# The feed-forward of a hybrid decoder block by one level of a Strassen scheme, up and down as two stages

## The chip, the cores and the metric

The kernel runs on one core of one Trainium2 chip. The metric is the device time of one execution in microseconds (us); of several runs the median is given. The core's engines each have a queue of their own and meet by semaphores: TensorE (PE) multiplies matrices into PSUM banks, VectorE (DVE), ScalarE (ACT) and GpSimd (POOL) work on tiles, and SyncE (SP) issues most of the DMAs.

## The reference, cut to what matters

The block has a norm, a wide input projection, three branches (a gated delta rule, a state space scan, a windowed attention), a gated merge and an output projection. The change lies behind all of these, in the last lines:

```python
h = h + merged @ w_out[l]
hn = rmsnorm(h, norm2_w[l])
h = h + jnp.square(jax.nn.relu(hn @ w_up[l])) @ w_down[l]
...
return rmsnorm(h, final_norm_w)[:, N_META:]
```

There are 1024 tokens (the meta tokens are not computed here), the model is 1024 wide and the feed-forward 4096, all in float32.

## The kernel before, in words

Every matmul operand is split into a high part, ScalarE's copy of the value in TensorE's fp32r type (`hi`, names that end in h), and the rest (`lo`, names that end in l); a product of two operands is three matmuls, hi x hi, hi x lo and lo x hi, that add up in one PSUM bank. A matmul here takes 128 partitions of both operands: 128 columns of the one by 512 of the other, into a bank of 128x512. Tokens come in two halves of 512, or eight tiles of 128 (NB = 8); the 1024 model channels in eight tiles of 128 (KT = 8) or two halves of 512; the 4096 channels of the feed-forward in 32 blocks of 128 (NFF = 32).

`stage_out` (L1083 on) makes h2, the residual with the output projection, in four rounds (token half `th`, column half `q`), each into four banks `pso` by 8 x 4 x 3 matmuls (L1108); VectorE adds each bank to h2 (L1112). In the round `th = 1, q = 0`, `mlp_in` is put between: for a token tile, ScalarE sums the squares (`row_scale`, L1125), VectorE adds and scales the sums (L1127, L1128) and takes the inverse (L1135), TensorE transposes the rows (`ups`, L1140), and ScalarE and VectorE make the transposed operand's hi and lo (L1144, L1145). The rows are not normalised for this; their factor `rs` is applied at the end, since the square of the relu scales with its square.

`stage_mlp` (L1148 on) goes over the 32 blocks two at a time, 16 passes. Up, 96 matmuls by `gemm` (L144): 2 blocks x 2 token halves x 3 x 8. Each of the four banks gets a relu (ACT, L1160), a square (DVE, L1161) and a split (ACT L1163, DVE L1164). Down, 96 matmuls (L1177): for each of 8 token tiles and 2 column halves, 2 blocks x 3; after each 6, VectorE adds the bank to h2, scaled by `rs` (L1179). Weights are split by ScalarE (L118, L131) and GpSimd (L120, L132). At the end `final_stats` and `final_apply` (L1197, L1204) normalise token tile by token tile and store; GpSimd makes the factor `rsf` as a power.

The order of the instructions on each engine is made by a scheduler with priorities and a cost model of its own; so the order in the source is not that on an engine, and the order is shown below. Tiles come from pools: a tag with a number of buffers, where a new tile waits until the last reader of the one before has ended. The eight PSUM banks are three pools: `mm` with three, `pc` with three, `pd` with two. A tag "y" has 32 buffers of 128x512, "m" 17, "d" 16, "t" and "r" four each; the eight h2 tiles are 128x1024. GpSimd's part in the merge and in the output projection (`wol`) is of the same form, L132.

## Time and profile before

| | us |
|---|---|
| median of three runs | 2766.83 (2761.62 to 2774.05) |
| the profiled execution | 2763.22 |
| its span, first to last instruction | 2761.5 |
| mean granted TensorE clock | 0.982 |
| up to the last round but one of the output projection | 1967.84 |
| last two rounds of the output projection | 48.3 |
| from there to the second pass of the feed-forward | 55.9 |
| the other passes, the norm and the stores | 689.5 |

From the second row on the times are those of the profiled execution. In its views each row has a start or a group, an engine, the line of the kernel and the names of the tiles (out<-in); "idle" in square brackets or behind the second bar is the time for which the engine waited before it, with what released it. A line L144 is that of the helper `gemm`; its tile's name, `up`, tells whose it is.

### The profile page before, as it was taken

The numbers are of one execution on the slowest core, as the hardware profiler recorded it, in microseconds if no ns is written. First come the engines' busy times: TensorE is split into PE (matmuls) and PEld (weight loads), VectorE is DVE, ScalarE is ACT, GpSimd is POOL, SyncE is SP. The second block draws the span as 40 slices with busy tenths as digits, with TensorE's granted clock in tenths as the row PEclk, the third lists the DMA queues.
The fourth block names the chain that finished last, engine by engine and source line by source line (L and its number), as shares of the span: only waits on it lengthen the run. The fifth ranks groups of instructions, "written<-read, shape, count | busy, mean of one in ns | idle before, by whom it ended". The sixth has DMA issues, their size and how long they took to land.

```text
span 2761.5 us, 36981 instructions
## 1 busy us (share of the span) xinstructions
PE 2629.8 (95%) x14367; PEld 2234.7 (81%) x14367; DVE 1456.6 (53%) x2775; ACT 906.1 (33%) x2385; POOL 696.3 (25%) x519
## 2 busy tenths in 40 slices
PE   6998999999999999999999999999999999999998
PEld 5887888888898898788878888888778777777776
DVE  5777766775665765576750122424254544444445
ACT  4434444443332332465541121212442121212122
POOL 3222222221232332322112222222432222222220
PEclk9989999998999999999999999999999999999999
DMA  3211121111112111322131131313221111111101
GB/s 120 64 42 53 52 60 52 53 44 49 47 62 85 62 62 62 88 61 63 47 122 46 54 106 46 107 53 114 90 73 54 39 53 44 50 47 51 47 16 69
DMA packets 88366, 172.94 MB, mean 63 GB/s; under 512 B 35862, under 2 KB 36278, under 8 KB 88190
## 3 DMA queue, kind: packets, MB, share of 16 engines
q1 hardware_dynamic: 83982, 162.81, 18.3%
q0 software_dynamic: 3200, 6.43, 1.1%
q8 instruction: 113, 1.85, 0.3%
q10 hardware_dynamic: 1008, 1.34, 0.1%
q14 instruction: 63, 0.52, 0.1%
HBM read 144.96 MB, written 19.14 MB: 59 GB/s over the span
## 4 chain that ended last, share of the span: by engine, by line
PE 75%; DVE 17%; issue 3%; ACT 2%; DMA 2%; POOL 1%; DVEq 0%; SPq 0%; POOLq 0%; ACTq 0%
PE up L144 13%; PE dn L1177 11%; PE mgm L144 9%; PE pr L1059 9%; PE pso L1108 3%; PE x L144 3%; PE gg L144 2%; PE aq L144 2%; PE v L144 2%; DVE xt L508 2%; PE z L144 2%; PE b L144 2%; PE q L144 1%; PE c L144 1%; PE k L144 1%
## 5 line engine op out<-in xcount | busy, mean ns | idle before, releaser
L1179 DVE SCALAR_TENSOR_TENSOR h<-dn,rs,h 128x512 f32<-128x512 f32 x256 | 191.9, 750 | 132.7 <-PE dn L1177 132.7
L1177 PE MATMUL dn<-wdh,ah 128*128 128x512 f32 x512 | 203.9, 398 | 14.9 <-DVE h L1179 14.9
L1161 DVE TENSOR_TENSOR ra<-ra 128x512 f32<-128x512 f32 x64 | 94.4, 1475 | 214.2 <-ACT ra L1160 214.2
L1177 PE MATMUL dn<-wdh,al 128*128 128x512 f32 x512 | 202.3, 395 | 0.0
L1177 PE MATMUL dn<-wdl,ah 128*128 128x512 f32 x512 | 202.2, 395 | 0.0
L1059 PE MATMUL pr<-yl,wph 128*128 128x512 f32 x384 | 150.1, 391 | 1.9 <-DVE yl L132 1.9
L1059 PE MATMUL pr<-yh,wph 128*128 128x512 f32 x384 | 150.1, 391 | 1.8 <-ACT wph L118 1.0
L132 POOL TENSOR_TENSOR wdl<-wdr,wdh 128x512 fp32r<-128x512 f32 x64 | 81.9, 1308 | 274.9 <-PE dn L1177 273.5
L1059 PE MATMUL pr<-yh,wpl 128*128 128x512 f32 x384 | 149.5, 389 | 0.0
L120 POOL TENSOR_TENSOR wul<-wur,wuh 128x1024 fp32r<-128x1024 f32 x32 | 76.6, 2393 | 249.7 <-PE up L144 246.7
L1177 PEld LDWEIGHTS dn<-wdh,ah 128*128 128x128 f32 x512 | 96.1, 188 | 45.6 <-DVE h L1179 23.9
L144 PE MATMUL up<-ul,wuh 128*128 128x512 f32 x512 | 129.0, 394 | 0.0
L144 PE MATMUL up<-uh,wul 128*128 128x512 f32 x512 | 128.4, 391 | 0.0
L144 PE MATMUL up<-uh,wuh 128*128 128x512 f32 x512 | 128.2, 391 | 0.0
L1069 DVE SCALAR_TENSOR_TENSOR gt<-gt,pr 128x512 f32<-128x512 f32 x32 | 21.9, 687 | 198.9 <-PE pr L1059 198.9
L131 ACT ACTIVATE wdh<-wdr 128x512 fp32r<-128x512 f32 x64 | 40.5, 633 | 255.5 <-PE dn L1177 246.6
L120 POOL TENSOR_TENSOR wpl<-wpr,wph 128x1024 fp32r<-128x1024 f32 x24 | 61.2, 2549 | 228.2 <-ACT wph L118 205.3
L1177 PEld LDWEIGHTS dn<-wdh,al 128*128 128x128 f32 x512 | 96.2, 188 | 23.3
L1177 PEld LDWEIGHTS dn<-wdl,ah 128*128 128x128 f32 x512 | 96.2, 188 | 21.8
L144 PEld LDWEIGHTS up<-ul,wuh 128*128 128x128 f32 x512 | 96.9, 190 | 20.0
L144 PEld LDWEIGHTS up<-uh,wul 128*128 128x128 f32 x512 | 96.4, 188 | 19.7
L144 PEld LDWEIGHTS up<-uh,wuh 128*128 128x128 f32 x512 | 96.1, 188 | 20.1
(422 smaller groups left out, 6563.2 us busy)
## 6 DMA issues: line engine op xcount, KB each, us to landing
wur<-in_wup SPq DMA_DIRECT2D x32, 512.0 KB
wdr<-in_wdn SPq DMA_DIRECT2D x64, 256.0 KB
mgr<-in_win SPq DMA_DIRECT2D x24, 512.0 KB
wpr<-in_wpr SPq DMA_DIRECT2D x24, 512.0 KB
yr<-yd SPq DMA_DIRECT2D x48, 256.0 KB
dms<-rowd SPq DMA_DIRECT2D x16, 512.0 KB
wor<-in_wout SPq DMA_DIRECT2D x32, 256.0 KB
gm<-rowd SPq DMA_DIRECT2D x8, 576.0 KB
```

The source lines that it names most:

```text
L120: nc.gpsimd.tensor_tensor(wl, wr, wh.bitcast(F32), op=ALU.subtract)
L131: nc.scalar.activation(h, r, AF.Copy)
L132: eng.tensor_tensor(l, r, h.bitcast(F32), op=ALU.subtract)
L144: nc.tensor.matmul(ps[:, 0:n], a[:, k, :], b[k][:, c0:c0 + n], start=(i == 0 and k == 0), stop=(i == 2 and k == KT - 1))
L508: nc.vector.tensor_tensor(tv, lb[:, j:j + 1, j + 1:32].broadcast_to([3 * n_, n, m]), ub[:, 0:n, j:j + 1].broadcast_to([3 * n_, n, m]), op= ...
L1059: nc.tensor.matmul(ps, x[:, k, :], y, start=(k == 0 and j == 0), stop=(k == KT - 1 and j == 2))
L1069: nc.vector.scalar_tensor_tensor(t, t, 1.0, ps, op0=ALU.add, op1=ALU.mult)
L1108: nc.tensor.matmul(ps, x[k, th][:, ts], y, start=(k == 0 and j == 0), stop=(k == KT - 1 and j == 2))
L1161: nc.vector.tensor_tensor(r, r, r, op=ALU.mult)
L1177: nc.tensor.matmul(ps, a[:, ts], b, start=(j == 0 and i == 0), stop=(j == G - 1 and i == 2))
L1179: nc.vector.scalar_tensor_tensor(self.h2[t][:, qs], ps, self.rs[:, t:t + 1], self.h2[t][:, qs], op0=ALU.mult, op1=ALU.add)
```

## The change

The two matrix products of the feed-forward become block products of 2 x 2 blocks, done with seven products in place of eight (Winograd's form of Strassen's scheme).

Up: two blocks of the feed-forward (a pair; 16 of them), two halves of the 1024 input channels, two halves of the tokens. A product is 12 matmuls of four channel tiles (`up_mm`); seven of them, `up1` to `up7`, make the four blocks c11, c12, c21, c22 of the pair. Their operands are sums and differences: of the activations, made once (`u_mix`, operand sets 0 to 6), and of the pair's weights, made anew for each pair (`ss`, `st`), on VectorE; all low parts of the up stage are made on VectorE. Since sums come after the transposes, the rows are now multiplied by their norm's factor before (`u_prep`: the power on GpSimd, the product on VectorE, L1169). Relu and square are both ScalarE's. The c's and four sums and differences of them, s1 to s4, seven tiles of 256 KB per pair, go to DRAM (`acd`) on SyncE's queue (`keep`, L1227). h2 is stored to DRAM (`hd`) and read back for the down stage, which gives its tiles to the weights. The first two products of pairs 0 and 1 are written ahead of `u_mix` (HOIST).

Down: three groups of 6, 5 and 5 pairs; in a group seven products, each a sum over its pairs, with operands read back from `acd` (L1357) and weights or differences of weights (`mix`); three of the seven make their weights' low part on GpSimd, the others on VectorE. A product fills four banks (one for each token tile of a half), 12 matmuls for each pair, and is then added to V, E7 or the h tiles (L1382). In the last product of all, the token tiles are the outer loop (`tail`).

The diff, cut to what is added in the place of `mlp_in` and of the body of `stage_mlp`, which calls `stage_up` and `stage_down` now; `h2tile`, `y2`, `m2`, `d2`, `t2` and `r2` take tiles of the tags above, `up_w1` loads a block of weights, `up_first` splits it, `up_hoist` does products 1 and 2, `relu2` is relu and square on ScalarE, `keep` stores to `acd`, `accum` adds four banks to each of the tiles that it is given (or, if `fresh`, copies them on ScalarE), and `bank` gives the four banks:

```diff
+NPR = NFF // 2
+HOIST = 2
...
+        self.acd = self.dram.tile([NPR, 7, P, 512], F32, name="acd")
+        self.hd = self.dram.tile([NB, P, D], F32, name="hd")
...
-                    if th == 1 and q == 0 and k % 2:
-                        self.mlp_in((k // 2,))
+                    if th == 1 and q == 0:
+                        if k == 0:
+                            self.u_prep(0)
+                        self.u_tile(0, k)
...
+    def split(self, src, hi, lo, eng=None):
+        nc = self.nc
+        nc.scalar.activation(hi, src, AF.Copy)
+        (eng or nc.vector).tensor_tensor(lo, src, hi.bitcast(F32), op=ALU.subtract)
+        return hi, lo
+    def u_prep(self, c):
+        nc = self.nc
+        self.hs = {}
+        for t in range(4 * c, 4 * c + 4):
+            nc.sync.dma_start(self.hd[t], self.h2[t])
+            r = self.final_stats(t)
+            if c:
+                w = self.h2tile("hs")
+                hs = [w[:, 0:512], w[:, 512:D]]
+            else:
+                hs = [self.y2("hs") for _ in range(2)]
+            for i in range(2):
+                nc.vector.tensor_scalar(hs[i], self.h2[t][:, 512 * i:512 * i + 512], r[:, 0:1], None, op0=ALU.mult)
+            self.hs[t % 4] = hs
+    def u_tile(self, c, k):
+        nc = self.nc
+        ps = self.pc("ups")
+        for t in range(4):
+            nc.tensor.transpose(ps[:, t * P:(t + 1) * P],
+                                self.hs[t][k // 4][:, (k % 4) * P:(k % 4 + 1) * P], self.ident)
+        n2 = self.cols[:, C_N2 + k:C_N2 + k + 1]
+        u = self.ur[c, k] = self.y2("u") if c == 0 else (self.t2 if k < 4 else self.r2)("u")
+        nc.scalar.activation(u, ps, AF.Copy, scale=n2)
+        if c == 0:
+            self.uo[0 if k < 4 else 1, k % 4] = self.split(u, self.y2("uh", F32R), self.y2("ul", F32R))
+    def u_mix(self):
+        nc = self.nc
+        b11, b12, b21, b22 = ([self.ur[c, 4 * i + k] for k in range(4)] for i in range(2) for c in range(2))
+        t2 = []
+        for k in range(4):
+            nc.vector.tensor_tensor(b11[k], b12[k], b11[k], op=ALU.subtract)
+        for k in range(4):
+            nc.vector.tensor_tensor(b12[k], b22[k], b12[k], op=ALU.subtract)
+        for k in range(4):
+            self.uo[2, k] = self.split(b22[k], self.y2("uh", F32R), self.y2("ul", F32R))
+            nc.vector.tensor_tensor(b22[k], b22[k], b11[k], op=ALU.subtract)
+            self.uo[5, k] = self.split(b22[k], self.m2("uh", F32R), self.d2("ul", F32R))
+        for k in range(4):
+            self.uo[4, k] = self.split(b11[k], self.m2("uh", F32R), self.d2("ul", F32R))
+        for k in range(4):
+            self.uo[6, k] = self.split(b12[k], self.m2("uh", F32R), self.d2("ul", F32R))
+        for k in range(4):
+            nc.vector.tensor_tensor(b21[k], b21[k], b22[k], op=ALU.subtract)
+            self.uo[3, k] = self.split(b21[k], self.m2("uh", F32R), self.d2("ul", F32R))
+    def up_mm(self, ps, w, p):
+        wh, wl = w
+        ops = [self.uo[p, k] for k in range(4)]
+        for j, (x, y) in enumerate(((wh, 0), (wh, 1), (wl, 0))):
+            for k in range(4):
+                self.nc.tensor.matmul(ps, x[:, k * P:(k + 1) * P], ops[k][y], start=(j == 0 and k == 0),
+                                      stop=(j == 2 and k == 3))
...
+    def up_pair(self, j, pre):
+        nc = self.nc
+        tt = nc.vector.tensor_tensor
+        w1 = self.up_w1(j)
...
+        if pre is None:
+            a11, a12 = self.up_first(w1)
+            pa = self.pd("up1")
+            self.up_mm(pa, a11, 0)
+        else:
+            pa, pb = pre
+        x1 = self.t2("x1")
+        nc.scalar.copy(x1, pa)
+        ss = self.h2tile("ss")
+        tt(ss[:, 0:512], a[2], a[3], op=ALU.add)
+        tt(ss[:, 512:D], ss[:, 0:512], a[0], op=ALU.subtract)
+        h, l = self.split(ss, self.h2tile("sh", dt=F32R), self.h2tile("sl", dt=F32R))
+        s1, s2 = (h[:, 0:512], l[:, 0:512]), (h[:, 512:D], l[:, 512:D])
+        if pre is None:
+            pb = bank("up2")
+            self.up_mm(pb, a12, 1)
+        c11 = self.y2("c11")
+        tt(c11, x1, pb, op=ALU.add)
+        self.relu2(c11, c11)
+        self.keep(j, 0, c11)
+        p6 = bank("up6")
+        self.up_mm(p6, s2, 5)
+        u2 = self.t2("u2")
+        tt(u2, x1, p6, op=ALU.add)
+        p5 = self.pc("up5")
+        self.up_mm(p5, s1, 4)
+        u4 = self.t2("u4")
+        tt(u4, u2, p5, op=ALU.add)
+        st = self.h2tile("st")
+        tt(st[:, 0:512], a[0], a[2], op=ALU.subtract)
+        tt(st[:, 512:D], a[1], ss[:, 512:D], op=ALU.subtract)
+        h, l = self.split(st, self.h2tile("sh", dt=F32R), self.h2tile("sl", dt=F32R))
+        s3, s4 = (h[:, 0:512], l[:, 0:512]), (h[:, 512:D], l[:, 512:D])
+        p7 = bank("up7")
+        self.up_mm(p7, s3, 6)
+        tt(u2, u2, p7, op=ALU.add)
+        c22 = self.y2("c22")
+        tt(c22, u2, p5, op=ALU.add)
+        self.relu2(c22, c22)
+        self.keep(j, 2, c22)
+        p3 = self.pc("up3")
+        self.up_mm(p3, s4, 2)
...
+        s = self.y2("s3")
+        tt(s, c11, c12, op=ALU.subtract)
+        self.keep(j, 5, s)
+        s = self.y2("s1")
+        tt(s, c12, c22, op=ALU.add)
+        self.keep(j, 3, s)
+        sq = self.y2("s2")
+        tt(sq, s, c11, op=ALU.subtract)
+        self.keep(j, 4, sq)
+        a22 = self.split(a[3], self.r2("wh", F32R), self.r2("wl", F32R))
+        p4 = self.pc("up4")
+        self.up_mm(p4, a22, 3)
+        c21 = self.y2("c21")
+        tt(c21, u2, p4, op=ALU.add)
+        self.relu2(c21, c21)
+        self.keep(j, 1, c21)
+        s = self.y2("s4")
+        tt(s, c21, sq, op=ALU.subtract)
+        self.keep(j, 6, s)
+    def stage_up(self):
+        self.u_prep(1)
+        pre = [self.up_hoist(0)]
+        for k in range(4):
+            self.u_tile(1, k)
+            self.u_tile(1, k + 4)
+        pre += [self.up_hoist(j) for j in range(1, HOIST)]
+        self.u_mix()
+        for j in range(NPR):
+            self.up_pair(j, pre[j] if j < HOIST else None)
+    def stage_down(self):
+        nc = self.nc
+        tt = nc.vector.tensor_tensor
+        V = [self.d2("V") for _ in range(4)]
+        E7 = [self.d2("E7") for _ in range(4)]
+        for t in range(NB):
+            self.h2[t] = self.h2tile(f"h3{t}")
+            nc.sync.dma_start(self.h2[t], self.hd[t])
...
+        for p0, n in ((0, 6), (6, 5), (11, 5)):
+            first, lastc = p0 == 0, p0 + n == NPR
...
+            for j in prs:
+                w = self.wst.tile([P, D], F32, name="wd1", tag=("wr", "wh", "wl")[nw % 3])
+                nw += 1
+                nc.sync.dma_start(w, self.I["wdn"][2 * j])
+                b1.append(w)
+            for j in prs:
+                for i, b in enumerate((b21, b22)):
+                    w = self.m2("wd2")
+                    nc.sync.dma_start(w, self.I["wdn"][2 * j + 1][:, 512 * i:512 * i + 512])
+                    b.append(w)
+            b11, b12 = [w[:, 0:512] for w in b1], [w[:, 512:D] for w in b1]
+            T1 = [self.y2("T1") for _ in prs]
+            def product(acc, ai, bs, mix=None, tail=False, eng=None):
+                ops = []
+                for i, j in enumerate(prs):
+                    if mix:
+                        mix(i)
+                    r = (self.t2 if i % 2 else self.r2)("ar")
+                    nc.sync.dma_start(r, self.acd[j, ai])
+                    ah, al = self.split(r, self.y2("ah", F32R), self.y2("al", F32R))
+                    wh, wl = self.split(bs[i], self.y2("wh", F32R), self.y2("wl", F32R), eng)
+                    ops.append((ah, al, wh, wl))
+                def mms(i, t):
+                    ah, al, wh, wl = ops[i]
+                    for m, (x, y) in enumerate(((ah, wh), (ah, wl), (al, wh))):
+                        nc.tensor.matmul(acc[t], x[:, t * P:(t + 1) * P], y,
+                                         start=(i == 0 and m == 0), stop=(i == n - 1 and m == 2))
...
+            ps = bank()
+            product(ps, 0, b11, eng=nc.gpsimd)
+            accum(ps, V, fresh=first)
+            accum(ps, C11)
+            ps = bank()
+            product(ps, 3, T1, mix=lambda i: tt(T1[i], b12[i], b11[i], op=ALU.subtract))
+            accum(ps, C12, C22)
+            ps = bank()
+            product(ps, 1, b21, eng=nc.gpsimd)
+            accum(ps, C11)
+            ps = bank()
+            product(ps, 6, b22, eng=nc.gpsimd)
+            accum(ps, C12)
+            ps = bank()
+            product(ps, 4, T1, mix=lambda i: tt(T1[i], b22[i], T1[i], op=ALU.subtract))
+            accum(ps, V)
+            if lastc:
+                for t in range(4):
+                    tt(C12[t], C12[t], V[t], op=ALU.add)
+            ps = bank()
+            product(ps, 5, b22, mix=lambda i: tt(b22[i], b22[i], b12[i], op=ALU.subtract))
+            accum(ps, E7, fresh=first)
+            if lastc:
+                fb = [self.d2("fnb") for _ in range(2)]
...
+                for t in range(4):
+                    tt(E7[t], E7[t], V[t], op=ALU.add)
+                    tt(C21[t], C21[t], E7[t], op=ALU.add)
+                    tt(C22[t], C22[t], E7[t], op=ALU.add)
+                for t in range(4):
+                    self.final_apply(t, self.final_stats(t), fb)
+            ps = bank()
+            product(ps, 2, b21, mix=lambda i: tt(b21[i], b21[i], T1[i], op=ALU.subtract), tail=lastc)
+            if not lastc:
+                accum(ps, C21)
+            else:
+                for t in range(4):
+                    tt(C21[t], C21[t], ps[t], op=ALU.add)
+                    self.final_apply(4 + t, self.final_stats(4 + t), fb)
```

How the order moves, at three places. First VectorE at the start of the up stage, where `ul` are low parts of the activations' sums, `st` a weight sum for product 7 of pair 0, `sl` its low part, and `wul`, `ss` belong to pairs 2 and 1:

```order
L1154 TENSOR_TENSOR ul_18785<-u_18294,uh_18784 128x512
L1154 TENSOR_TENSOR ul_18790<-u_18323,uh_18789 128x512
L1201 TENSOR_TENSOR u_18352<-u_18352,u_18668 128x512
L1262 TENSOR_TENSOR c11_18811<-x1_18802,up2_18601 128x512
L1268 TENSOR_TENSOR u2_18829<-x1_18802,up6_18816 128x512
L1154 TENSOR_TENSOR ul_18795<-u_18352,uh_18794 128x512
L1272 TENSOR_TENSOR u4_18844<-u2_18829,up5_18831 128x512
L1274 TENSOR_TENSOR st_18846<-wu1_18798,wu2_18800 128x512
L1275 TENSOR_TENSOR st_18846<-wu1_18798,ss_18804 128x512
L1154 TENSOR_TENSOR wl_18899<-wu2_18800,wh_18898 128x512
L1154 TENSOR_TENSOR sl_18850<-st_18846,sh_18849 128x1024
L1154 TENSOR_TENSOR wul_19053<-wu1_19048,wuh_19052 128x1024
```

Before, VectorE has only the second token half's low parts (`ul`, L1145) here; the sums and their low parts are new.

Second, SyncE between the last store of the up stage and the first operands of the down stage; before, SyncE here only has the weights of the passes, in turn:

```order
L116 DMA wur_21317<-in_wup 128x1024
L116 DMA wur_21323<-in_wup 128x1024
L129 DMA wdr_21749<-in_wdn 128x512
L129 DMA wdr_21755<-in_wdn 128x512
L129 DMA wdr_21761<-in_wdn 128x512
L129 DMA wdr_21767<-in_wdn 128x512
```

And now:

```order
L1227 DMA acd_98<-c21_21210 128x512
L1227 DMA acd_98<-s4_21215 128x512
L1346 DMA wd2_21266<-in_wdn 128x512
L1346 DMA wd2_21268<-in_wdn 128x512
L1346 DMA wd2_21270<-in_wdn 128x512
L1346 DMA wd2_21272<-in_wdn 128x512
L1346 DMA wd2_21274<-in_wdn 128x512
L1346 DMA wd2_21276<-in_wdn 128x512
L1357 DMA ar_21288<-acd_98 128x512
L1357 DMA ar_21298<-acd_98 128x512
```

The weight loads of the down stage stand ahead of the first operand `ar`, and that one reads from `acd`, which the rows above it write.

Third, VectorE at the end of the down stage. Before, the additions of the last pass alternate with the norm's work:

```order
L1179 SCALAR_TENSOR_TENSOR h_17702<-dn,rs_18104,h_17702 128x512
L1127 TENSOR_TENSOR ssm<-ss_23445 128x1
L1204 SCALAR_TENSOR_TENSOR h_17698<-h_17698,rsf,fnb 128x512
L1179 SCALAR_TENSOR_TENSOR h_17702<-dn,rs_18104,h_17702 128x512
L1128 TENSOR_SCALAR ssm<-ssm 128x1
L1204 SCALAR_TENSOR_TENSOR h_17698<-h_17698,rsf,fnb 128x512
```

Now the low parts of the last product's operands 1 to 4 (`al`, `wl`) stand behind the additions to E7 and to the h tiles, which wait for the product ahead of it:

```order
L1416 TENSOR_TENSOR E7_21223<-E7_21223,V_21219 128x512
L1416 TENSOR_TENSOR E7_21224<-E7_21224,V_21220 128x512
L1417 TENSOR_TENSOR h35_21236<-h35_21236,E7_21223 128x512
L1418 TENSOR_TENSOR h35_21236<-h35_21236,E7_21223 128x512
L1417 TENSOR_TENSOR h36_21238<-h36_21238,E7_21224 128x512
L1418 TENSOR_TENSOR h36_21238<-h36_21238,E7_21224 128x512
L1416 TENSOR_TENSOR E7_21225<-E7_21225,V_21221 128x512
L1154 TENSOR_TENSOR al_24046<-ar_24043,ah_24045 128x512
L1417 TENSOR_TENSOR h37_21240<-h37_21240,E7_21225 128x512
L1418 TENSOR_TENSOR h37_21240<-h37_21240,E7_21225 128x512
L1154 TENSOR_TENSOR wl_24050<-wd2_23199,wh_24049 128x512
L1154 TENSOR_TENSOR al_24057<-ar_24054,ah_24056 128x512
```

The E7 rows that begin this chain (L1382, four of them) stand a few rows higher, and five more low parts follow.

More of the change, by code (lines that the diff above doesn't have):

```diff
@@ L1112, in stage_out @@
                     nc.vector.scalar_tensor_tensor(sl, ps, 0.5, sl, op0=ALU.mult, op1=ALU.add)
-                if th == 0 and q == 1:
-                    self.u = [[[self.half("y", 4 * KT, n) for n in ("uh", "ul")] for k in range(KT)]
-                              for c in range(2)]
-                    self.rs = self.lp.tile([P, NB], F32, name="rs2")
-        self.mlp_in(range(4, 8))
     def row_scale(self, t):
@@ new lines, in h2tile, with y2, m2, d2 @@
+    def h2tile(self, name, shape=(P, D), dt=F32):
+        return self.rp.tile(list(shape), dt, name=name, tag="h2", bufs=NB)
+    def y2(self, name, dt=F32):
+        return self.half("y", 4 * KT, name, dt)
+    def m2(self, name, dt=F32):
+        return self.half("m", NM, name, dt)
+    def d2(self, name, dt=F32):
+        return self.half("d", 2 * KT, name, dt, self.rp)
+    def t2(self, name, dt=F32):
+        return self.half("t", 4, name, dt, self.tp)
+    def r2(self, name, dt=F32):
+        return self.half("r", 4, name, dt)
@@ new lines, in up_mm, with up_w1 @@
+    def up_mm(self, ps, w, p):
[5 more added lines that the diff above has]
+                                      stop=(j == 2 and k == 3))
+    def up_w1(self, j):
+        w1 = self.wst.tile([P, D], F32, name="wu1", tag="wr")
+        self.nc.sync.dma_start(w1, self.I["wup"][2 * j])
+        return w1
@@ new lines, in up_first, with relu2, keep, up_hoist @@
+    def up_first(self, w1):
+        h, l = self.split(w1, self.wst.tile([P, D], F32R, name="wuh", tag="wh"),
+                          self.wst.tile([P, D], F32R, name="wul", tag="wl"))
+        return (h[:, 0:512], l[:, 0:512]), (h[:, 512:D], l[:, 512:D])
+    def relu2(self, dst, src):
+        self.nc.scalar.activation(dst, src, AF.Relu)
+        self.nc.scalar.activation(dst, dst, AF.Square)
+    def keep(self, j, i, src):
+        self.nc.sync.dma_start(self.acd[j, i], src)
+    def up_hoist(self, j):
+        pa = self.pd("up1")
+        a11, a12 = self.up_first(self.up_w1(j))
+        self.up_mm(pa, a11, 0)
+        pb = self.pmm.tile([P, 512], F32, name="up2", tag="mm", bufs=3)
+        self.up_mm(pb, a12, 1)
+        return pa, pb
@@ L1194, in final_stats @@
+    def stage_mlp(self):
+        self.stage_up()
+        self.stage_down()
     def final_stats(self, t):
```

100 lines of the change are left out of this document (40 added, 60 removed).

## Prediction

> **What bounds the kernel now.** I read the page's first and fourth part, then the chain of waits, then groups of instructions. The page gives busy time by engine and the chain's shares:
>
> ```profile
> PE 2629.8 (95%) x14367; PEld 2234.7 (81%) x14367; DVE 1456.6 (53%) x2775; ACT 906.1 (33%) x2385; POOL 696.3 (25%) x519
> PE 75%; DVE 17%; issue 3%; ACT 2%; DMA 2%; POOL 1%; DVEq 0%; SPq 0%; POOLq 0%; ACTq 0%
> ```
>
> TensorE is busy 95% of the span and holds 75% of the chain; VectorE is busy only 53%. The change touches the feed-forward, so its stretch matters. The chain there, in order of time (start, us, what):
>
> ```profile
> 1995.97 18.10 PE pso L1108 x79
> 2016.16 4.16 DVE ssm L1127
> ...
> 2072.02 21.80 PE up L144 x96
> ...
> 2253.76 21.80 PE up L144 x96
> 2276.26 2.35 DVE ra L1161
> 2279.33 19.86 PE dn L1177 x84
> 2299.19 21.80 PE up L144 x96
> ```
>
> One pass over two of the 32 blocks goes from 2253.76 to 2299.19, 45.43 us, for 192 matmuls. The windows view of the steady stretch (sum, then busy time of PE, PEld, DVE, ACT, POOL, then granted clock, DMA share, GB/s) says the same:
>
> ```profile
> 2072.02:2708.09 636.07, 622.17 (x2690) 502.82 (x2689) 290.09 (x336) 131.43 (x193) 137.04 (x83) 1.00 0.14 44
> ```
>
> TensorE is busy 622 of 636 us at full clock, the other engines less than half, the DMA 14%. Only fewer matmuls shorten this stretch, and the change takes away one in eight.
>
> **The gain.** Before, 16 passes have 192 matmuls each. After, each pair of blocks has 7 products of 12 matmuls in the up stage and 84 in the down stage: 168. In the chain an up matmul takes 21.80/96 = 0.2271 us, and one of the down projection 19.86/84 = 0.2364. The new up stage has the old one's form: 84 x 0.2271 = 19.1 us a pair. The new down stage sends three matmuls to a bank and then goes to the next of four, with no eviction between; nearest is the output projection, which does the same: 18.10/79 = 0.2291, so 84 x 0.2291 = 19.2 us. Per pair 38.3 instead of 45.43, 7.1 less; times 16, **-114 us** (-117 with the down stage at 0.2271, -104 at 0.2364).
>
> **Does TensorE stay the bound in the up stage?** The groups that price the new work:
>
> ```profile
> L1161 DVE TENSOR_TENSOR ra<-ra 128x512 f32<-128x512 f32 x64 | 94.4, 1475 | 214.2 <-ACT ra L1160 214.2
> L1164 DVE TENSOR_TENSOR al<-ra,ah 128x512 fp32r<-128x512 f32 x64 | 44.3, 693 | 33.0 <-ACT ah L1163 32.5
> L1069 DVE SCALAR_TENSOR_TENSOR gt<-gt,pr 128x512 f32<-128x512 f32 x32 | 21.9, 687 | 198.9 <-PE pr L1059 198.9
> L627 DVE TENSOR_TENSOR vt<-vt,f 128x1024 f32<-128x1024 f32 x8 | 9.8, 1226 | 13.9 <-POOL f L626 13.9
> L205 DVE TENSOR_SCALAR xn<-xt,xrs 128x1024 f32<-128x1024 f32 x4 | 3.0, 742 | 1.3 <-POOL xrs L201 1.3
> L131 ACT ACTIVATE wdh<-wdr 128x512 fp32r<-128x512 f32 x64 | 40.5, 633 | 255.5 <-PE dn L1177 246.6 <-DMA wdr<-in_wdn 6.1
> L1160 ACT ACTIVATE ra<-up 128x512 f32<-128x512 f32 x64 | 38.3, 598 | 178.5 <-PE up L144 178.5
> L118 ACT ACTIVATE wuh<-wur 128x1024 fp32r<-128x1024 f32 x32 | 33.9, 1060 | 24.7 <-PE up L144 24.7
> ```
>
> A pair gives VectorE 16 operations of 128x512 at 0.69 and three of 128x1024 at 1.23: 14.7 us. ScalarE has three hi parts at 1.06, one at 0.63 and nine copies, relus and squares at 0.60: 9.2 us. Both are under 19.1. In the order of the changed kernel, VectorE makes the weight sums of pair j+1 between the evictions of pair j, so TensorE never waits for a sum of its own pair. SyncE has seven stores and two loads a pair, 2.75 MB in 19.1 us or 144 GB/s, where a window of the clock's table below has 264. In the up stage GpSimd does almost nothing, which matters because of the first row's mean, 1475 against 693. The timeline shows both cases:
>
> ```profile
> 2265.39 0.69 DVE L1161 TENSOR_TENSOR ra<-ra 128x512 f32<-128x512 f32 x1 [3.35 <-ACT ra L1160]
> 2270.23 2.39 POOL L120 TENSOR_TENSOR wul<-wur,wuh 128x1024 fp32r<-128x1024 f32 x1 [12.95 <-PE up L144]
> 2270.83 2.35 DVE L1161 TENSOR_TENSOR ra<-ra 128x512 f32<-128x512 f32 x1 [3.36 <-ACT ra L1160]
> ```
>
> Alone it takes 0.69; beside a GpSimd operation it ends only after that one. An operation with a PSUM operand (L1069, 687 ns) isn't held up. I take 19.1 us for a pair.
>
> **The start of the up stage.** Before, from 2016.16 to 2072.02 are 55.9 us, of which 45.4 are a pass: 10.4 us over. After, two waits come. First, in the last output rounds TensorE transposes rows that are normalised already, so it waits for Squares, sums, a power and two multiplications:
>
> ```profile
> L1125 ACT ACTIVATE sqm<-h 128x512 f32<-128x512 f32 x32 | 20.0, 627 | 12.8 <-DVE ssm L1127 4.4 <-DVE ssm L1128 3.5 <-DVE h L1179 3.0
> L1125 ACT ACTIVATION_READ_ACCUMULATOR sqm<-h 128x1 f32 x32 | 6.0, 187 | 0.0
> L1127 DVE TENSOR_TENSOR ssm<-ss 128x1 f32<-128x1 f32 x16 | 6.6, 411 | 3.1 <-ACT sqm L1125 3.0
> L1128 DVE TENSOR_SCALAR ssm<-ssm 128x1 f32<-128x1 f32 x16 | 2.4, 150 | 0.3
> L1197 POOL TENSOR_TENSOR rsf<-ssm,pneg 128x1 f32<-128x1 f32 x8 | 5.5, 689 | 64.6 <-DVE ssm L1128 64.6
> L132 POOL TENSOR_TENSOR wol<-wor,woh 128x512 fp32r<-128x512 f32 x32 | 41.8, 1310 | 57.1 <-ACT woh L131 57.1
> ```
>
> For the last token tile: 2 x (0.63 + 0.19) + 0.41 + 0.15 + 0.69 + 2 x 0.37 = 3.6 us, and a wol of 1.31 may stand ahead on GpSimd. I take **+3.5** (0 if queued matmuls cover it, 6 with two wols). Second, the activations' combinations. The four last token tiles need 4 x 1.63 us of Squares on ScalarE, then 0.56 + 0.69 + 0.74, with 0.7 for the eviction ahead (it reads PSUM, like L1069): 9.2; a transposed round and its copy 1.2 more. Then 46 operations stand on VectorE in order until the low part for product 7 of pair 0: 44 x 0.69 + 2 x 1.23 = 32.8. So product 7 starts 43 us after the output projection, and eight products of the two first pairs follow, 96 matmuls or 21.8 us: 65 us, of which two pairs are 38.1. 27 us over against 10.4 before: **+16.6** (+8 if half of VectorE's row is done earlier than I think, +26 if the second pair's loads, which stand in SyncE's row behind pair 0's first store, come late). The hoisted products of pairs 0 and 1 are in the 43.
>
> **From up to down.** SyncE issues the last store, six weight loads, and only then the first read of what was stored. The merge stage's loads of the same 256 KB from DRAM price it; the issue rate is that of the loads of x:
>
> ```profile
> 1890.75 3.83 SPq L1088 DMA_DIRECT2D h<-in_x  x8
> ```
> ```profile
> 1425.89 4.51 DMA yr<-yd
> 1431.81 3.78 DMA yr<-yd
> 1437.68 3.46 DMA yr<-yd
> ```
>
> After the last product: sum 0.69, relu and square 1.2, s4 0.69, together 2.6; seven issues of 3.83/8 = 0.48, 3.4; the landing 4.5; the hi part 0.63: **+11.1** (8 if the landing takes 3.5 and issues go ahead, 16 if the 1.8 MB ahead drain first). The later operands follow at 0.48 us and are used at 2.7 us each, so they don't wait.
>
> **The down stage.** A group of six pairs has 118 operations of 0.69 on VectorE, 81 us, and 504 matmuls, 115 us; of five, 77 and 96. GpSimd makes 48 low parts of 1.31 in all. Added whole to VectorE (24 and 20 us a group) they come to 105 and 97: level with TensorE in the groups of five. **+3** (0 if the look-ahead of five to six items hides it, 25 if two fifths of the 63 us of holds land on the path). The Trainium skill, "SBUF — State Buffer", says of the port pair that the two engines share that it is an exclusive lock, that only VectorE operations with two SBUF inputs meet it here, and that whoever starts second waits in full. The three timeline rows and L1069 agree; by that rule alone the accumulations, which read PSUM, are never held, and this term would be 0 as long as the look-ahead covers the low parts.
>
> **The end.** In VectorE's order the low parts of the last product's operands 1 to 4 stand behind the sums that wait for the product ahead of it. From that product's end the last low part is the 24th operation: 24 x 0.69 = 16.6 us; 31 matmuls are then left, 7.1. Undisturbed the product is 60 x 0.229 = 13.7. 16.6 + 7.1 - 13.7 = **+10** (4 if more is ready, 15 since two operand loads also stand behind eight output stores). The tail:
>
> ```profile
> 2751.87 0.40 PE L1177 MATMUL dn<-wdh,al 128*128 128x512 f32 x1
> 2757.08 1.41 DVE L1204 SCALAR_TENSOR_TENSOR h<-h,rsf,fnb 128x512 f32<-128x512 f32 x2 [0.72 <-POOL rsf L1197]
> ```
>
> Before, 9.2 us from the last matmul to 2761.5. After, for one token tile: 0.69 + 1.63 + 0.56 + 0.69 + 1.41 and the same 3.0 of storing: 8.0, **-1**.
>
> **The clock.** A wait of TensorE in the timeline, and windows of 2 us around its end, with the columns as above:
>
> ```profile
> 2021.49 0.33 PE L1140 MATMUL ups<-ident,h 128*128 128x128 f32 x1 [3.88 <-DVE ssm L1128]
> ```
> ```profile
> 2020.00:2022.00 2.00, 0.51 (x3) 0.47 (x4) 1.82 (x9) 0.15 (x1) 0.30 (x1) 1.00 0.72 264
> 2022.00:2024.00 2.00, 2.00 (x9) 1.48 (x8) 1.31 (x6) 1.88 (x7) 0.00 (x0) 0.65 0.40 137
> 2024.00:2026.00 2.00, 2.00 (x8) 1.51 (x7) 0.60 (x4) 1.46 (x7) 0.00 (x0) 0.50 0.00 0
> 2026.00:2028.00 2.00, 2.00 (x11) 1.44 (x9) 1.07 (x6) 1.02 (x4) 0.00 (x0) 1.00 0.00 0
> ```
>
> After 3.88 us idle the granted clock is 0.65 and 0.50 for two windows: 0.7 + 1.0 = 1.7 us lost, about 2. The change has three more such waits: **+6** (2 to 8).
>
> **The sum.** -114 + 3.5 + 16.6 + 11.1 + 3 + 10 - 1 + 6 = -65. The profiled execution took 2763.2 us (span 2761.5); 2763.2 - 65 = 2698. The median of the runs lies 3.6 above that execution: **2702 us**. The terms' bounds, which seldom fall all to one side, make 2684 to 2728 of it.
>
> **The rivals.** *Almost the whole gain.* The lower bounds hold at the seams and TensorE fills them: -117 + 8 + 8 + 4 + 2 - 1 = -96, **2671**. For it: seven eighths of the matmuls are all the chain needs. Against: the orders show VectorE's and SyncE's rows as they are.
>
> *No change.* All 48 low parts of GpSimd in the down stage come onto the path, 48 x 1.31 = 63 us, and use up the 65: **2765**. For it: L1161 at 1475 instead of 693, and the sums of five pairs being level. Against: only three of seven products use GpSimd, and accumulations read PSUM, like L1069.
>
> *Slower: the up stage at VectorE's pace.* If its 22 units of a pair cost what L1161 does on average, 22 x 1.475 = 32.5 us, a pair takes 13.4 more than TensorE's 19.1; 14 pairs, +188: **2890**. It decides from 19.1 + 65/14 = 23.7 us a pair. Against: that mean comes from GpSimd, which is idle there.
>
> *Slower: the clock falls at every product of the down stage.* If each of the 21 products begins with a wait like the one of 3.88 us, it costs that and some 2 us of half clock: 21 x 5.9 = 124, **2826**; it decides from 11 of them. Against: operands are made five to six items ahead. The Trainium skill, "TensorE: Matmul & The Clock Gate", describes such an oscillation for matmul bursts that each wait for a load (the section on HAM oscillation); in this trace only single waits show it.
>
> That the matmuls aren't saved I rule out: the changed order has 84 a pair in each stage.
>
> **How the numbers follow.** Forecast 0.68, almost the whole gain 0.17, no change 0.07, slower by VectorE 0.04, slower by the clock 0.04. The first two and their bounds give the range 2664 to 2742, leaving out the rest and their fringes. About 0.5% (14 us) is what a measurement of this kernel can tell from no change: faster 0.85, same 0.07, slower 0.08.
>
> **What would show it.** Right: two products of pairs 2 to 15 in the chain 19.1 us apart from pair to pair; TensorE idle once some 11 us before the first down matmul, some 25 us in pieces before pair 2, some 10 us in the last product. Wrong: pairs over 20 us in the up stage; VectorE's two-input operations above 0.69 there; TensorE idle at most product changes of the down stage; down matmuls over 0.235.

## The result and the profile after

| | before | after | ratio, 95% interval |
|---|---|---|---|
| first measurement, median of four runs each (us) | 2765.05 | 2701.54 | 0.976 [0.973, 0.979] |
| the changed kernel again, median of eleven (before) and six runs | 2769.64 | 2697.73 | 0.973 [0.970, 0.976] |
| profiled execution of the first measurement, span | 2761.5 | 2698.7 | |
| from the output projection's first matmul to the end | 838.3 | 766.6 | |

The change is faster by 2.4 to 2.7%. The forecast was 2702, but the last row of the table says that this is a little too good to be true: the part of the program that the change touches became 72 us shorter, not 65, and the part ahead of it, whose code is the same, happened to take 9 us longer in the profiled execution of after. The first matmul of the output projection in the two timelines, before and after:

```profile
1923.21 0.39 PE L1108 MATMUL pso<-woh,mh 128*128 128x512 f32 x1
```
```profile
1932.12 0.39 PE L1115 MATMUL pso<-woh,mh 128*128 128x512 f32 x1
```

In the fourteen traces of this study that matmul begins between 1923 and 1944 us, whatever the kernel. So all that follows is measured from it; two traces of each kernel agree on that stretch within 1 us (838.3 and 839.2 before, 766.6 and 766.5 after).

The page of after, first and fourth part:

```profile
PE 2547.8 (94%) x13983; PEld 2178.5 (81%) x13983; DVE 1608.3 (60%) x3039; ACT 1034.7 (38%) x2581; POOL 614.7 (23%) x479
PE 75%; DVE 16%; issue 3%; DMA 2%; ACT 2%; POOL 1%; ACTq 0%; SPq 0%; DVEq 0%; POOLq 0%
```

TensorE has 384 matmuls less and is still the engine that is always busy; VectorE went up by 152 us and isn't the bound. The chain of waits through the feed-forward (start, us, what) shows its new form, two long runs of TensorE with a few waits at the seams, the places where one stage hands over to the next:

```profile
2027.84 1.80 DVE h L1119 x3
2051.90 5.32 DVE ul L1154 x9
2064.47 291.96 PE up L1209 x1260
2364.08 4.60 DMA wd<-in_wdn
2368.74 5.01 DMA ar<-acd
2375.10 291.63 PE dn L1365 x1274
2677.80 6.76 PE dn L1365 x22
```

TensorE's timeline at the beginnings of two pairs of the up stage, and then at its end and the seams that follow:

```profile
2204.86 1.07 PE L1209 MATMUL up<-uh,wuh 128*128 128x512 f32 x4
2224.13 1.07 PE L1209 MATMUL up<-uh,wuh 128*128 128x512 f32 x4
```
```profile
2064.47 2.07 PE L1209 MATMUL up<-uh,sh 128*128 128x512 f32 x4 [5.65 <-ACT sh L1153]
...
2358.12 1.09 PE L1209 MATMUL up<-uh,wl 128*128 128x512 f32 x4
2373.74 0.80 PE L1365 MATMUL dn<-wh,ah 128*128 128x512 f32 x1 [14.53 <-ACT wh L1153]
2375.10 0.80 PE L1365 MATMUL dn<-wl,ah 128*128 128x512 f32 x1 [0.56 <-POOL wl L1154]
...
2677.80 0.79 PE L1365 MATMUL dn<-wl,ah 128*128 128x512 f32 x1 [5.42 <-DVE wl L1154]
...
2689.15 0.39 PE L1365 MATMUL dn<-wh,al 128*128 128x512 f32 x1
```

A pair takes 2224.13 - 2204.86 = 19.27 us, and so do the pairs around it. The up stage ends at 2359.04 (the last four matmuls begin at 2358.12, 0.23 apart). The numbers in brackets are TensorE's waits: 5.65 for the first pair's weight sums (four of 0.75 to 2.01 stand ahead of it), 14.53 before the down stage, 5.42 in its last product; the down stage has no other above 0.6. Two windows, one pair of the up stage and the steady part of the down stage (sum, then PE, PEld, DVE, ACT, POOL, granted clock, DMA share, GB/s):

```profile
2166.31:2185.59 19.28, 19.28 (x86) 15.77 (x85) 13.64 (x19) 9.02 (x14) 0.00 (x0) 1.00 0.38 150
```
```profile
2380.00:2640.00 260.00, 260.00 (x1147) 215.36 (x1146) 212.27 (x304) 117.01 (x205) 65.37 (x45) 1.00 0.44 142
```

TensorE fills both; a matmul takes 260/1147 = 0.2267 us in the second. VectorE has 5.6 us of a pair to spare in the up stage, and 48 of 260 us in the down stage.

### The profile page after: what moved, and what is told of

The parts are those of the page before. It is cut to its first block, busy times and chain, and to the rows that moved or that the text cites. A ratio compares the mean times of both kernels' runs of the same rounds, so it can differ in the third digit from the quotient of the medians.

```text
span 2698.7 us, 37432 instructions
## 1 busy us (share of the span) xinstructions
PE 2547.8 (94%) x13983; PEld 2178.5 (81%) x13983; DVE 1608.3 (60%) x3039; ACT 1034.7 (38%) x2581; POOL 614.7 (23%) x479
## 4 chain that ended last, share of the span: by engine, by line
PE 75%; DVE 16%; issue 3%; DMA 2%; ACT 2%; POOL 1%; ACTq 0%; SPq 0%; DVEq 0%; POOLq 0%
PE dn L1365 11%; PE up L1209 11%; PE mgm L148 9%; PE pr L1063 9%; PE pso L1115 3%; PE aq L148 3%; PE x L148 3%; PE gg L148 2%; PE v L148 2%; PE q L148 2%; DVE xt L512 2%; PE z L148 2%; PE b L148 2%; PE c L148 2%; PE k L148 1%
## 5 line engine op out<-in xcount | busy, mean ns | idle before, releaser
L1365 PE MATMUL dn<-wh,ah 128*128 128x512 f32 x448 | 175.5, 393 | 14.5 <-ACT wh L1153 14.5
L1365 PE MATMUL dn<-wl,ah 128*128 128x512 f32 x448 | 176.2, 394 | 6.0 <-DVE wl L1154 5.4
L1365 PE MATMUL dn<-wh,al 128*128 128x512 f32 x448 | 175.6, 392 | 0.0
L1154 DVE TENSOR_TENSOR al<-ar,ah 128x512 fp32r<-128x512 f32 x112 | 98.7, 884 | 51.3 <-ACT ah L1153 51.1
L1365 PEld LDWEIGHTS dn<-wh,ah 128*128 128x128 f32 x448 | 85.1, 190 | 32.9 <-ACT wh L1153 15.0
L1365 PEld LDWEIGHTS dn<-wl,ah 128*128 128x128 f32 x448 | 85.1, 190 | 24.7 <-DVE wl L1154 6.1
L148 PE MATMUL mgm<-hnh,mgh 128*128 128x512 f32 x384 | 100.1, 398 | 2.1 <-ACT gt L1047 2.1
L148 PE MATMUL mgm<-hnl,mgh 128*128 128x512 f32 x384 | 99.9, 399 | 0.0
L148 PE MATMUL mgm<-hnh,mgl 128*128 128x512 f32 x384 | 99.5, 396 | 0.0
L1365 PEld LDWEIGHTS dn<-wh,al 128*128 128x128 f32 x448 | 85.2, 190 | 17.7
```

Source lines behind the costliest of these rows:

```text
L148: nc.tensor.matmul(ps[:, 0:n], a[:, k, :], b[k][:, c0:c0 + n], start=(i == 0 and k == 0), stop=(i == 2 and k == KT - 1))
L1154: (eng or nc.vector).tensor_tensor(lo, src, hi.bitcast(F32), op=ALU.subtract)
L1365: nc.tensor.matmul(acc[t], x[:, t * P:(t + 1) * P], y, start=(i == 0 and m == 0), stop=(i == n - 1 and m == 2))
```

## The experiments

The theory: TensorE is the bound in both stages, so each loses what its matmuls lose; what is given back stands at the seams, and each seam is the order of one engine's row. The rivals were VectorE as the bound of the up stage, GpSimd's holds on VectorE in the down stage, and transfers. All differences below are of the stretch from the output projection's first matmul to the end, against 766.6 us of the changed kernel, which takes the chance of the stages ahead out. Each comes from one trace of the edited kernel.

**Undo one half: the down stage with eight plain products.**

```diff
-            product(ps, 0, b11, eng=nc.gpsimd)
-            accum(ps, V, fresh=first)
...
+            for ai, bs, C, eng in ((0, b11, C11, nc.gpsimd), (0, b12, C12, None), (1, b21, C11, nc.gpsimd),
+                                   (1, b22, C12, None), (3, b11, C21, nc.gpsimd), (3, b12, C22, None),
+                                   (2, b21, C21, nc.gpsimd), (2, b22, C22, None)):
...
+                product(ps, ai, bs, eng=eng, tail=last)
...
-        tt(s, c11, c12, op=ALU.subtract)
-        self.keep(j, 5, s)
```

> The down stage with eight plain block products in place of seven, and without the sums s1 to s4; the up stage stays as changed. If the time of the down stage is that of its matmuls: 16 x 12 = 192 more at 0.227 us, +43.6 us, less up to 7 us because the sums at the end go, so about 37 to 44 us over the changed kernel (2738 to 2745). If the stage is paced by its loads or by VectorE and GpSimd, the seven products have not gained so much and it is under +20 us (below 2722).

Measured: 2739.87, the stretch 810.3, **+43.7**. The 192 matmuls more are 43.5 at 0.2266. Its waits sit elsewhere (7.0 us in the first product, and 10.0 in the fifth of the last group's eight, where this version puts the loads of the operands behind the stores of finished tokens) but sum to 18.9 us against 20.5. The down stage is paced by its matmuls, and its share of the gain is nearly whole.

**Undo the other half: the up stage with eight plain products.**

```diff
+                ps = self.pmm.tile([P, 512], F32, name="up", tag="mm", bufs=3)
+                for m, (x, y) in enumerate(((0, 0), (0, 1), (1, 0))):
+                    for k in range(KT):
+                        nc.tensor.matmul(ps, ws[k // 4][x][:, (k % 4) * P:(k % 4 + 1) * P],
+                                         self.uo[7 * c + k // 4, k % 4][y], start=(m == 0 and k == 0),
...
-        self.u_mix()
```

> The up stage with eight plain block products (96 matmuls a pair), without the sums of activations and weights; the stores and the down stage stay as changed. If the start of the up stage pays for the sums: 21.8 for 19.27 us a pair, +40, and the start goes from 22.8 us over two pairs back to about 10.6, -12, so about +28 us over the changed kernel (2730). If the start's waits come from something else (the norm, the transposes, the loads), +40 (2742).

Measured: 2716.82, the stretch 780.95, **+14.4**, less than either number. The up stage itself, from the end of the output projection, takes 355.7 us for 331.2: +24.5, near the +28, of which the pairs, 21.91 us each, are +42.2 and the start -17.7; its start has no wait over 0.4. The other 10 us come back at the seam to the down stage:

```profile
2385.20 2.00 PE L1213 MATMUL up<-uh,wul 128*128 128x512 f32 x8
2389.58 0.60 PE L1285 MATMUL dn<-wh,ah 128*128 128x512 f32 x1 [2.39 <-ACT wh L1153]
```

There TensorE waits 2.4 us where the changed kernel waits 14.5. So of the 42 us that fewer matmuls save in the up stage, two thirds go for the start and the seam; the sums cost more than I had put down for the start alone, and of the 58 us that the two halves bring one by one, three quarters are the down stage's. The other 14 of the 72 belong to neither alone. Two plain stages together weren't run, but the traces say where such a remainder comes from. Before, the 96 down matmuls of a pass took 45.43 - 21.80 = 23.63 us with their waits; in the new form 96 of them take 96 x 0.2266 = 21.75, which is 30 us less over 16 passes (a plain up pair takes 2 us more in all than before, 21.91 for 21.80). So of the 114 us that the pairs gain, some 86 (42.2 + 43.5) come from seven products in place of eight, and the other 28 from giving the down projection a stage of its own; by this estimate eight products would have had those 28 too, and paid the seams for them.

**Double the suspect: more sums on VectorE.** The four weight sums are repeated, 18 and then 6 operations more a pair:

```diff
         tt(ss[:, 0:512], a[2], a[3], op=ALU.add)
+        tt(ss[:, 0:512], a[2], a[3], op=ALU.add)
...
         tt(st[:, 0:512], a[0], a[2], op=ALU.subtract)
+        tt(st[:, 0:512], a[0], a[2], op=ALU.subtract)
...
```

> Each pair of the up stage repeats its four weight sums, 18 more operations of 128x512 on VectorE; the results are the same. If TensorE is the bound at 19.27 us and VectorE has room: its row a pair is 13.2 us at the spacing of 0.61 (14.7 at 0.69), so with 18 more 24.2 to 27, and the pairs take that: +4.9 to +8 us a pair, +70 to +110 us. If VectorE's row already sets the pace, all 18 count: 18 x 0.61 x 16 = +176 us. If nothing but TensorE counts, 0.

Measured: 2860.04, the stretch 929.2, **+162.6**: more than the theory's 70 to 110 and nearly the rival's 176. A window of two pairs:

```profile
2120.51:2178.32 57.81, 43.90 (x169) 34.34 (x169) 49.50 (x75) 18.68 (x27) 0.00 (x0) 0.88 0.27 100
```

VectorE is busy 24.75 us a pair, as reckoned, but the pair takes 28.9: the repeated sums stand between the evictions, a weight sum and with it its high part `sh` come late, and TensorE waits 7 us in each pair, some 5.5 of them at once, and then runs its 84 matmuls in 22 us instead of 19.3, since the granted clock is 0.88 on the mean. That is the falling clock of my last rival, in the up stage. The run doesn't tell slack from pace, so the smaller dose:

> The test of VectorE's room again, with 6 more sums of weights a pair in place of 18; the results are the same. VectorE is busy 13.6 us of 19.27 in a pair; six more are 3.7 us, so 17.3. If TensorE is the bound, 0 to +6 us in all (the first pair waits for VectorE). If VectorE's row with its waits already sets the pace, as the 28.9 us a pair of the run with 18 more would also allow, +3.7 us a pair, +59 us.

Measured: 2712.61, the stretch 781.1, **+14.5**. The steady pairs:

```profile
2100.00:2200.00 100.00, 100.00 (x432) 80.13 (x432) 86.90 (x128) 46.86 (x66) 0.00 (x0) 1.00 0.39 147
```

TensorE is busy all the time; VectorE 87%; a pair takes 19.53 for 19.27. So TensorE is the bound, with the room on VectorE that the sums said; not +59. But +14.5 is above the 0 to +6 of the theory as well. Some 5 of it are a longer start (the wait before the first pair's sums is 20.1 us in place of waits of 11.2 in all), which the expectation had too small; the pairs are 4, two waits in the last pair 3, and the down stage 2.

**GpSimd taken out of the down stage.**

```diff
-            product(ps, 0, b11, eng=nc.gpsimd)
+            product(ps, 0, b11)
-            product(ps, 1, b21, eng=nc.gpsimd)
+            product(ps, 1, b21)
-            product(ps, 6, b22, eng=nc.gpsimd)
+            product(ps, 6, b22)
```

> The 48 low parts that GpSimd makes in the down stage are made by VectorE. If GpSimd holds VectorE up and VectorE has room without it: VectorE's row in a group of six is 136 x 0.61 to 0.69 = 83 to 94 us against 115 of TensorE, so no change but the start of the stage, 0 to -3 us. If GpSimd's share is what keeps VectorE below TensorE, it gets slower, +5 us or more.

Measured: 2705.26, the stretch 765.4, **-1.2**: inside the theory's 0 to -3, and little more than two traces of one kernel differ by. The 48 holds were hidden, and GpSimd's help wasn't needed.

**The same two engines at the start of the up stage.**

```diff
-            self.uo[4, k] = self.split(b11[k], self.m2("uh", F32R), self.d2("ul", F32R))
+            self.uo[4, k] = self.split(b11[k], self.m2("uh", F32R), self.d2("ul", F32R), nc.gpsimd)
...
```

> Twelve low parts of the activations' sums at the start of the up stage go from VectorE to GpSimd; nothing else changes. If the two engines exclude each other for operations with two SBUF operands, eight of the twelve at 1.31 us come on top of VectorE's remaining 33 rows of 0.61 before product 7 of pair 0: it starts 0 to 4 us later than in the changed kernel. If they run side by side, VectorE's row is 13 shorter and it starts 4 to 8 us earlier.

Measured: 2704.96, the stretch 771.6, **+5.0**. GpSimd's and VectorE's timelines there:

```profile
2057.35 17.80 POOL L1154 TENSOR_TENSOR ul<-u,uh 128x512 fp32r<-128x512 f32 x12 [18.36 <-ACT uh L1153]
```
```profile
2067.09 0.69 DVE L1262 TENSOR_TENSOR c<-x,up 128x512 f32<-128x512 f32 x1 [6.86 <-ACT x L1252]
2067.72 0.69 DVE L1268 TENSOR_TENSOR u<-x,up 128x512 f32<-128x512 f32 x1
2068.32 7.91 DVE L1154 TENSOR_TENSOR sl<-st,sh 128x1024 fp32r<-128x1024 f32 x1
2076.16 0.67 DVE L1272 TENSOR_TENSOR u<-u,up 128x512 f32<-128x512 f32 x1
```

In the middle of GpSimd's row, `c` and `u`, which read one operand from PSUM, take 0.69 as ever. `sl`, with both operands in SBUF, takes 7.91 us where it takes 1.23 alone, and ends 1 us after GpSimd's last operation: it was held through all that GpSimd had left, the rest of one operation and five more. It goes the other way too. GpSimd's first operation began among VectorE's operations with two SBUF operands, which ran on to 2060.24, and ended 1.2 us behind them, after 4.05 us for 1.31:

```profile
2057.35 4.05 POOL L1154 TENSOR_TENSOR ul<-u,uh 128x512 fp32r<-128x512 f32 x1 [18.36 <-ACT uh L1153]
```

Product 7 began 1.7 us earlier than in the changed kernel, which neither range had (0 to 4 later, 4 to 8 earlier), and then waited 4.7 us for `sl`. This is the shared port pair as the Trainium skill has it ("SBUF — State Buffer", "Terms", on that port pair), with one difference: the page has the lock held for the full instruction, and here the loser waited through the whole row of instructions that its neighbour had ready.

**The seam to the down stage: loads early.**

```diff
+        for i in range(4):
+            r = (self.t2 if i % 2 else self.r2)("ar")
+            nc.sync.dma_start(r, self.acd[i, 0])
+            ar0.append(r)
         for t in range(NB):
             self.h2[t] = self.h2tile(f"h3{t}")
```

> The first four operands of the down stage are asked for at its head, so they stand in SyncE's row among the stores of pairs 13 to 15, ahead of the last ten weight loads; nothing else moves. If the wait of 14.5 us is the order of SyncE's row (last store, six weight loads, then the operand's landing), it goes to 3 us or less and the half clock behind it goes too: -12 to -15 us over the changed kernel. If the wait is the transfers themselves (359 to 402 GB/s in that stretch), the operands come as late as before or the weights do: 0 to -4 us.

Measured: 2692.91, the stretch 759.5, **-7.1**, between the two. TensorE and ScalarE at the seam:

```profile
2359.42 1.09 PE L1209 MATMUL up<-uh,wl 128*128 128x512 f32 x4
2364.84 0.53 PE L1373 MATMUL dn<-wh,ah 128*128 128x512 f32 x1 [4.33 <-ACT wh L1153]
```
```profile
2363.12 0.63 ACT L1224 ACTIVATE c<-c 128x512 f32<-128x512 f32 x1
2363.66 0.61 ACT L1153 ACTIVATE ah<-ar 128x512 fp32r<-128x512 f32 x1
2364.18 0.61 ACT L1153 ACTIVATE wh<-wd 128x512 fp32r<-128x512 f32 x1
```

The wait fell by 10.2 us, so it was the order of SyncE's row and the load's landing. But the operands now lie ready while ScalarE still has the last pair's relu and square ahead of them in its row: 4.3 us stay. The clock falls all the same (0.50 until 2372), and the down stage takes 3 us more. Next in line was an engine's row that I hadn't listed.

**The last product: operands first.**

```diff
+            last = None
+            if lastc:
+                last = product(None, 2, b21, mix=lambda i: tt(b21[i], b21[i], T1[i], op=ALU.subtract), go=False)
             accum(ps, E7, fresh=first)
...
-            product(ps, 2, b21, mix=lambda i: tt(b21[i], b21[i], T1[i], op=ALU.subtract), tail=lastc)
+            product(ps, 2, b21, mix=lambda i: tt(b21[i], b21[i], T1[i], op=ALU.subtract), tail=lastc, ops=last)
```

> The operands of the very last product are written ahead of the additions to E7 and the h tiles, so that their low parts stand before these in VectorE's row. If the stall of 5.4 us in the last product is VectorE's order, it goes and with it 1.7 us of half clock: -6 to -7 us over the changed kernel. If the additions then come late for the norm and the stores, the tail takes it back: 0 to -2 us.

Measured: 2691.71, the stretch 760.5, **-6.1**. TensorE has no wait left there; the down stage is 7.3 us shorter, and the tail 1.4 longer, because the sums now run beside the last product.

**The first pair: weight sums first.**

```diff
+        sums = self.up_sums(0)
         self.u_mix()
         for j in range(NPR):
-            self.up_pair(j, pre[j] if j < HOIST else None)
+            self.up_pair(j, pre[j] if j < HOIST else None, None if j else sums)
```

(`up_sums` holds pair 0's loads, `ss`, `st` and their splits, taken out of `up_pair`.)

> The weight sums of pair 0 (ss, st and their low parts) are made ahead of the activations' combinations, so product 7 of pair 0 needs 12 rows of VectorE less. If that wait of 5.65 us is VectorE's order, it goes, and with it the half clock of the next two products (about 2 us): -6 to -8 us over the changed kernel. If product 7 then waits for the activations' low parts in its turn, 0 to -2 us.

Measured: 2695.09, the stretch 760.4, **-6.2**. The wait of 5.65 is gone; those ahead of it grew from 5.6 to 8.4 us in all.

**All edits together, beside the changed kernel.**

> The changed kernel again, unedited: its time beside that of the edits, and a second trace. If the 8.9 us by which the output projection began later in the first trace of the changed kernel than in that of before are chance (the seven traces so far have it between 1923 and 1940), the stretch from the output projection's first matmul to the end is again 766 to 767 us, and its start is anywhere in that range.

> The edits of the three seams together (loads early, operands of the last product first, weight sums of pair 0 first), and the down stage's low parts all on VectorE. If the seams are separate, their stretches add: -7.1 - 6.1 - 6.2 - 1.2 = -20.6 us over the changed kernel, about 2681. If one edit only moves the next one's wait, less than -14.

Measured: the changed kernel 2697.73, its stretch 766.5, its start at 1930.8; all edits **2678.28**, ratio to before 0.967 [0.964, 0.969], the stretch 746.2, -20.4. The seams add up as single ones do. It is the fastest version here, 3.3% under before. The kernel before a second time:

> The kernel before again, unedited, for a second trace. If the stages ahead of the change vary by chance, their end (the output projection's first matmul) lies anywhere between 1923 and 1940 us here too, while the stretch from there to the end is 838.3 us as in the first trace. If the first trace of before was typical and the change moved the stages ahead of it, it begins at 1923 again.

Measured: 2784.98 in one run; the output projection begins at 1944.2 and the stretch is 839.2. So the first trace of before lay at the early end by chance, and the 9 us have nothing to do with the change.

## Why the prediction was right, point by point

| term | predicted | measured |
|---|---|---|
| the matmuls' time, 16 pairs | -114 | -114.1 |
| wait for normalised rows | +3.5 | +3.0 |
| start of the up stage | +16.6 | +12.2, with the clock's loss |
| up to down | +11.1 | +15.3 |
| down stage, between products | +3 | 0 |
| last product | +10 | +5.4 |
| tail | -1 | -0.1 |
| half clock | +6 | +5.1 in the down stage |
| sum | -65 | -73 |

- **Gain.** A pair takes 19.27 + 84 x 0.2266 = 38.3 us, as forecast, by two small errors that cancel: up matmuls at 0.2294 instead of 0.2271, down matmuls at 0.2266 instead of 0.2291. Of the 114 some 28 aren't due to the number of matmuls, by the estimate from the two plain stages; the sum had them in it, by its cheaper down matmul, but "Only fewer matmuls shorten this stretch" was too narrow.
- **TensorE stays the bound.** VectorE was reckoned at 14.7 us a pair and is busy 13.6; ScalarE at 9.2 and is 9.0. The runs with more sums and the plain stages agree.
- **Wait for normalised rows.** Output projection 95.8 for 92.8 us, three waits of 0.42, 1.76 and 1.19.
- **Start of the up stage.** Product 7 begins at 2064.47, 36.6 us after the output projection (2027.88) and not 43. It begins on the high part `sh`; the low part `sl`, to which the prediction counted, ended 1.2 us later, ahead of its use. Operations with a duration of 0.69 follow each other every 0.605 us when none waits, so the row of 46 is 28.9 instead of 32.8; the norm ahead of it took 7.7 for 10.4. From product 7 to pair 2 are 24.8 us, not 21.8, for half clock. In all 61.3 for 65, or 22.8 over two pairs of 19.27, against 10.6 before. Twelve such operations in VectorE's timeline, with 7.31 us for all:

```profile
2051.82 7.31 DVE L1154 TENSOR_TENSOR ul<-u,uh 128x512 fp32r<-128x512 f32 x12
```

- **Up to down.** Undersized: 14.7 us from the end of the last matmul, and 0.6 for the first low part, for 11.1. The path was right, but three of its four steps were too short. The last store is issued 4.2 us after the last matmul and not 2.6, since the sums s3, s1 and s2 stand ahead of c21's in VectorE's row. From there to the first operand's issue are 3.4, as forecast. That operand lands 5.9 us after its issue, not 4.5. Then two high parts, `ah` and `wh`, take 1.2, where I had one at 0.63. VectorE's, SyncE's and ScalarE's timelines:

```profile
2359.84 0.69 DVE L1297 TENSOR_TENSOR s<-s,c 128x512 f32<-128x512 f32 x1
2360.44 0.68 DVE L1303 TENSOR_TENSOR c<-u,up 128x512 f32<-128x512 f32 x1
2363.20 0.32 SPq L1227 DMA_DIRECT2D acd<-s  x1
2363.57 2.97 SPq L1346 DMA_DIRECT2D wd<-in_wdn  x6
2366.59 3.28 SPq L1357 DMA_DIRECT2D ar<-acd  x5
2372.54 0.63 ACT L1153 ACTIVATE ah<-ar 128x512 fp32r<-128x512 f32 x1 [10.09 <-DMA ar<-acd]
2373.07 0.61 ACT L1153 ACTIVATE wh<-wd 128x512 fp32r<-128x512 f32 x1
```

  The two landings behind each other in the chain of waits, 4.60 and 5.01, are a later operand's: the chain comes to them through GpSimd's `wl`, and TensorE's wait of 14.53 ended with `wh`. The DMA engines were full there, which I had only in the upper bound of 16 (window of 2 us, the last two columns are the DMA share and GB/s):

```profile
2372.00:2374.00 2.00, 0.26 (x1) 0.26 (x1) 0.69 (x1) 1.46 (x3) 0.23 (x1) 0.50 1.05 402
```

- **Down stage.** Nothing between products; the look-ahead covers the holds, which was the lower end and what the rule of the shared port gave.
- **Last product.** The mechanism was right, and its size half: I let TensorE wait for the last low part, but it takes the operands in turn and only waits for the first one it lacks (`wl` at 2677.06), while the others arrive under its matmuls. VectorE's timeline, with that one and the last:

```profile
2677.06 0.69 DVE L1154 TENSOR_TENSOR wl<-wd,wh 128x512 fp32r<-128x512 f32 x1
...
2680.67 0.69 DVE L1154 TENSOR_TENSOR wl<-wd,wh 128x512 fp32r<-128x512 f32 x1
```

- **The measured sum** is -73; the stretch shows -71.7, since before the last pass ends 1.4 us ahead of sixteen full ones. That the median came out at 2702 all the same is luck, by the stages ahead of the change: measured again, the two medians differ by 71.9.

The rivals: VectorE didn't become the bound, but with 18 operations a pair more its row sets the pace, at 28.9 us a pair; the clock doesn't fall between products of the down stage (it is at 1.00 from 2380.6 to 2677.5); GpSimd's holds cost about 1 us at most.

## What to carry to other kernels

Where TensorE is busy through a long steady stretch, fewer matmuls give their full time back (here some 86 us for 384), if the other engines' rows per step are counted and stay under it; what is lost is at the seams, once each, and each seam is one engine's row in which what is needed first stands behind what is needed later. A seam's wait is worth more than its length, since the clock comes back only some microseconds behind it (3.1 in the last product, 6.8 at the seam to the down stage). Compare two traces from a point behind the last unchanged stage: here that took away a difference of up to 21 us that had nothing to do with the edit.
